# Expert rows by indirect transfers and transposes instead of one-hot products

## The chip, the core and the metric

The kernel runs on one core of one Trainium2 chip. The metric is device time in microseconds (us) of one execution; the median of three runs before is 2757.31 us (2755.22 to 2757.72). The engines are TensorE (PE; PEld is its weight load), VectorE (DVE), ScalarE (ACT), GpSimd (POOL) and SyncE (SP), which issues nearly all transfers. PSUM is the memory that PE writes to; SBUF is the on-chip memory that all engines read and write.

## What is computed

The reference runs two transformer layers (`first_block`) and then a hybrid layer. Each of the first two has a hierarchical mixture of experts (MoE) on 512 tokens of D = 1024, with 32 experts in 4 groups, hidden size 256, and two experts for each token:

```python
g_logits = (t @ w_rg) + b_rg                     # 4 groups
g_sel = argmax(g_logits); g_p = softmax(g_logits)[g_sel]
e_prob = softmax(e_logits[rows, g_sel])          # 8 experts of that group
top_p, top_i = top_k(e_prob, 2)
gates = g_p * top_p / sum(top_p)
...
hid = silu(xb @ w_gate[e]) * (xb @ w_up[e])      # xb: the rows of t sent to expert e
ys  = (hid @ w_down[e]) * slot_gate
out = segment_sum(ys, slot_tok)                  # back to the tokens
```

`t` is the RMS-normed hidden state. The rest of the model (attention, the gate behind the MoE, the last layer) is not touched by the change.

## The kernel before

Slots and groups. `moe_route` (L935) works out, for each token and each of its two experts, a slot number ("position"); blocks of 64 slots belong to one expert. The first 33 blocks are taken in 17 groups of two blocks (the last has one); two groups make a pair `u` of 256 slots. Blocks past those go through `moe_overflow` (L1349), a loop that makes no passes with these inputs; but its entry is a place where all engines meet.

Getting the rows. `router` leaves four scaled tiles `xg`, and for each a high and a low part `hs` (ACT's `copyH`, DVE's `subL`; for tiles 2 and 3 the latter at L1055, at the end of the routing). For a pair, `gather_oh` (L1133) makes a one-hot `OH` (DVE, four tiles of 128 tokens x 256 slots, two operations each, L1145 and L1146). `gather_rows(u, kk)` (L1166) multiplies `hs` by it: 16 products of 256 columns into a PSUM tile "z", copied by ACT to `X` (L1178), which has the rows turned (features on partitions, slots on columns). Four of these make a pair.

Steps. `moe` (L1059) runs a list of steps: an "up" multiplies X by the gate and up weights of a group (16 f32 products, `mm<-wu,X` in the trace), a "down" by its down weights (8 f32 products of 512 columns, `z<-wh,hid` or `z<-raw,hid`). After the first few, ups are odd steps and downs even ones. In between stand small jobs that `at(step, ...)` puts ahead of a step: the gates of a pair (`gather_gates`, PSUM tag "tp"), the transposes of its one-hots (`back`, "tp"), the transposes of the hidden state (`hidden`, "tp"), a quarter of `gather_rows`, and `combine` (L1222), which multiplies a down's outputs by turned one-hots into the PSUM tag "o", after which DVE adds it to the hidden state (L1230). "tp" and "o" have one buffer each, "z" two. Two combines stand ahead of each step from step 6 on. The order of PE, ACT, DVE and POOL in this part is the order in which the code is written; nothing reorders it:

```python
with self.tc.manual_schedule(engines={ET.PE, ET.Activation, ET.DVE, ET.Pool}):
    for s in range(N + 8):
        for f in todo.pop(s, ()):
            f = f()
            if callable(f):
                f()
        if s < N and steps[s]:
            work(s)
```

Behind each product step `rows` puts ACT's copy (L240) and DVE's subtraction (L253), which split a down's output in high and low parts. The expert weights come by SP's queue in the order of the program, into a ring of six 1 MB tiles ("wu") and the rings "wh" and "raw"; a load waits until PE has used the tile's last content. The first of them behind the loop's entry is L1114.

Of the kernel before, what the change touches and what calls it, by code (L numbers as in the profile page):

```python
# [12 lines left out]
I32 = mybir.dt.int32  # L13
AF = mybir.ActivationFunctionType
# [91 lines left out]
class Kern:  # L106
# [756 lines left out]

    def router(self, l, xs):
# [16 lines left out]
        hs = []  # L881
# [27 lines left out]
        def then(c, tt):  # L909
# [25 lines left out]
    def moe_route(self, l, xs):  # L935
# [19 lines left out]
        for tt in (2, 3):  # L955
            self.after(nc.scalar.activation(hs[tt][0], xg[tt], AF.Copy, scale=r[:, tt:tt + 1]), first)
# [68 lines left out]
        G = self.t("gates", [128, 4, 4], bufs=1)  # L1025
        v.reduce_sum(G[:, :, 2:4].rearrange("p t i -> p i t"), Ef, axis=AX.X)

# [25 lines left out]
        last = v.tensor_sub(GHL[:, :, 1], d, GHL[:, :, 0].bitcast(F32))  # L1053
        for tt in (2, 3):
            self.after(v.scalar_tensor_tensor(hs[tt][1], xg[tt], r[:, tt:tt + 1], hs[tt][0].bitcast(F32), op0=OP.mult,  # L1055
                                              op1=OP.subtract), last)
        return hs, G, GHL, oe, it

    def moe(self, l, xs):  # L1059
# [19 lines left out]
        hs, G, GHL, oe, it = self.moe_route(l, xs)  # L1079
# [49 lines left out]
        OHs, GSs, Xs, SG, Y, OHT, HID, PS = {}, {}, {}, {}, {}, {}, {}, {}  # L1129
# [4 lines left out]

        def gather_oh(u, tt):

            if tt == 0:
                pr = G[:, :, 2:4]
                if u > 0:
                    pr = self.small([128, 4, 2])  # L1140
                    nc.vector.tensor_scalar(pr, G[:, :, 2:4], -256.0 * u, None, op0=OP.add)
                OHs[u] = self.F4([128, 4, 256], F32R, "g"), pr
            OH, pr = OHs[u]
            io = self.c["iota"]
            v.tensor_scalar(OH[:, tt], io, pr[:, tt, 0:1], None, op0=OP.is_equal)  # L1145
            v.scalar_tensor_tensor(OH[:, tt], io, pr[:, tt, 1:2], OH[:, tt].bitcast(F32), op0=OP.is_equal, op1=OP.add)  # L1146

# [872 lines left out]
```

## Time and profile before

| | |
|---|---|
| median of 3 runs | 2757.31 us |
| profiled execution, device time | 2758.76 us |
| its span | 2756.7 us |
| mean granted TensorE clock | 0.975 of 2.4 GHz |
| PE / DVE / ACT / POOL busy | 2602.7 / 1338.8 / 1002.9 / 318.6 us |
| moved by transfers | 383.55 MB, mean 139 GB/s |

The MoE's expert steps take about 478 to 810 us of the span in the first layer and 1342 to 1670 in the second. The page gives busy times over the whole span; the tables of stretches and the timelines below are of single places in the expert steps, where the limits can be seen. A row of a timeline gives start, length, engine, line, operation, output<-input, count, and in brackets the idle time before it and what ended that.

### The profile page before, as it was taken

The page shows a single profiled execution, that of the slowest core. Times are in us where ns is not written, and L with a number is a line of the kernel's source. Part 1 is how long each engine was busy: PE and PEld are TensorE (multiplying, and loading weights), DVE is VectorE, ACT ScalarE, POOL GpSimd, SP SyncE. Part 2 cuts the span into 40 slices and gives each one's busy share as a digit, 9 for nine tenths or more (in the row PEclk, how much of TensorE's full clock was granted, in tenths as well). Part 3 has the DMA queues.
Part 4 walks back from the last instruction along what each step waited for, and adds up shares of the span by engine and source line. Part 5 has one row for each costly group of instructions (what it writes and reads, how often), then busy time and mean ns, then how long its engine had stood idle before and what let it go on. Part 6 is the DMA issues. An engine that isn't in the chain of part 4 may idle for free. (4 is left out here: it accounts for less than half of the span.)

```text
span 2756.7 us, 37138 instructions
## 1 busy us (share of the span) xinstructions
PE 2602.7 (94%) x14711; PEld 2000.0 (73%) x14711; DVE 1338.8 (49%) x2557; ACT 1002.9 (36%) x1840; POOL 318.6 (12%) x381
## 2 busy tenths in 40 slices
PE   7989998999999988999799999899999999999998
PEld 6777786555559777789455557777776688888898
DVE  6786535233357687644433336654356612533323
ACT  4654333211134564433111115444554522322222
POOL 0120011000000121012000001110003552011101
PEclk9999998999999999999899999999998999999999
DMA  5111336788833211223798853322121233233321
GB/s 170 54 54 62 87 126 209 291 326 314 327 114 115 77 46 47 86 93 123 268 341 314 332 210 116 119 71 60 49 73 58 89 95 119 85 99 92 96 92 66
DMA packets 224769, 383.55 MB, mean 139 GB/s; under 512 B 19658, under 2 KB 162599, under 8 KB 224592
## 3 DMA queue, kind: packets, MB, share of 16 engines
q1 hardware_dynamic: 224592, 381.13, 40.8%
q8 instruction: 118, 1.93, 0.3%
q14 instruction: 59, 0.48, 0.1%
HBM read 374.23 MB, written 6.85 MB: 138 GB/s over the span
## 5 line engine op out<-in xcount | busy, mean ns | idle before, releaser
L253 DVE TENSOR_TENSOR wh<-raw,wh 128x1024 fp32r<-128x1024 f32 (+1 forms) x251 | 304.5, 1214 | 468.7 <-ACT wh L240 464.3
L285 PE MATMUL mm<-f,wh 128*128 128x512 f32 x1296 | 525.8, 407 | 5.9 <-DVE q L251 4.7
L287 PE MATMUL mm<-f,wh 128*128 128x512 f32 x1296 | 512.5, 396 | 0.0
L286 PE MATMUL mm<-f,wh 128*128 128x512 f32 x1296 | 512.2, 395 | 0.0
L240 ACT ACTIVATE wh<-raw 128x1024 fp32r<-128x1024 f32 (+1 forms) x278 | 290.1, 1046 | 450.5 <-PE mm L286 284.6
L285 PEld LDWEIGHTS mm<-f,wh 128*128 128x128 f32 x1296 | 246.4, 190 | 72.1 <-issue 11.1
L287 PEld LDWEIGHTS mm<-f,wh 128*128 128x128 f32 x1296 | 246.0, 190 | 52.3 <-issue 0.5
L286 PEld LDWEIGHTS mm<-f,wh 128*128 128x128 f32 x1296 | 246.8, 190 | 45.9 <-issue 1.0
L1062 PE MATMUL mm<-wu,X 128*64 128x512 f32 x928 | 205.8, 596 | 0.0
L1062 PE MATMUL z<-g,o 128*128 128x256 f32 (+1 forms) x1152 | 153.9, 288 | 17.8 <-DVE g L1146 17.8
L1062 PEld LDWEIGHTS z<-g,o 128*128 128x128 f32 x1152 | 146.3, 194 | 22.1 <-DVE g L1146 18.0
L1062 PEld LDWEIGHTS mm<-wu,X 128*64 128x64 f32 x928 | 64.0, 137 | 120.4 <-issue 118.1
L1062 PE MATMUL o<-q,g 128*128 128x512 f32 x448 | 129.7, 411 | 5.7 <-DVE q L1230 5.3
L1230 DVE TENSOR_TENSOR q<-q,o 128x512 f32<-128x512 f32 x112 | 76.6, 684 | 105.5 <-PE o L1062 105.5
L1062 PEld LDWEIGHTS o<-q,g 128*128 128x128 f32 x448 | 75.7, 188 | 55.2 <-issue 34.1
L285 PE MATMUL mm<-wh,q 128*128 128x256 f32 x384 | 111.2, 290 | 3.7 <-ACT q L240 3.7
L1200 DVE SCALAR_TENSOR_TENSOR gs<-gs,mm 128x256 f32<-128x256 f32 x32 | 13.5, 422 | 205.7 <-ACT gs L444 205.7
L287 PE MATMUL mm<-wh,q 128*128 128x256 f32 x384 | 109.2, 284 | 2.7 <-POOL q L253 2.6
L286 PE MATMUL mm<-wh,q 128*128 128x256 f32 x384 | 108.5, 283 | 0.0
L253 POOL TENSOR_TENSOR wh<-raw,wh 128x1024 fp32r<-128x1024 f32 (+1 forms) x27 | 80.4, 2987 | 182.6 <-ACT wh L240 182.6
L1178 ACT COPY X<-z 128x512 f32<-128x512 f32 (+1 forms) x72 | 40.5, 563 | 156.3 <-PE z L1062 156.3
L253 DVE TENSOR_TENSOR q<-z,q 128x1024 fp32r<-128x1024 f32 x32 | 39.2, 1225 | 109.7 <-ACT q L240 109.7
(444 smaller groups left out, 4833.5 us busy)
## 6 DMA issues: line engine op xcount, KB each, us to landing
raw<-in_w_in_dram SPq DMA_DIRECT2D x142, 512.0 KB
wu<-in_w_exp_gate_dram SPq DMA_DIRECT2D x116, 512.0 KB
wu<-in_w_exp_up_dram SPq DMA_DIRECT2D x116, 512.0 KB
wh<-in_w_exp_down_dram SPq DMA_DIRECT2D x76, 512.0 KB
raw<-in_w_exp_down_dram SPq DMA_DIRECT2D x56, 512.0 KB
raw<-in_w_gu_dram SPq DMA_DIRECT2D x44, 512.0 KB
raw<-in_w_down_dram SPq DMA_DIRECT2D x20, 512.0 KB
raw<-in_w_o_dram SPq DMA_DIRECT2D x16, 512.0 KB
```

The lines of the kernel that those rows point to most:

```text
L240: nc.scalar.activation(o, i, AF.Copy, scale=scale)
L253: e.tensor_sub(o, i, h)
L285: mm(ps, aH, bH, start=first, stop=False, skip_group_check=True)
L286: mm(ps, aH, bL, start=False, stop=False, skip_group_check=True)
L287: mm(ps, aL, bH, start=False, stop=last, skip_group_check=True)
L1062: mm = lambda *a, **k: nc.tensor.matmul(*a, **k, skip_group_check=True)
L1178: return lambda: nc.scalar.copy(Xs[u][:, kk * 2:kk * 2 + 2, 0:n], pz[:, :, 0:n])
L1200: v.scalar_tensor_tensor(sg[r], sg[r], 1.0, pa[r, 0], op0=OP.add, op1=OP.mult)
L1230: return lambda: v.tensor_add(xs[tt][:, cs], xs[tt][:, cs], po)
```

## The change

`hs` is now a tile of 512 rows x 1024 in DRAM. `row_tile` scales `xg` with ACT into a tile and writes it there through POOL's queue (four times 512 KB for a layer). `row_numbers` multiplies the one-hots by the column of token numbers (8 f32 products of one column for a pair, into the tag "tp"), and DVE casts the result to integers. `row_gather` lets POOL fetch 128 rows of 4 KB by that list (an indirect transfer) into an SBUF tile, and `turned(g)` turns them with 8 transposes into a "z" tile, which ACT copies to `X` in one operation. The high and low parts and their DVE subtractions are gone. One-hots and gathers of the first pair are issued inside `moe_route`, right behind the positions, those of the second pair ahead of the overflow loop; later pairs' one-hots at steps 4u-8 and 4u-7, their row numbers and gathers at 4u-6, the turns at 4u-2 and 4u. The one-hots move from the SBUF tag "g" to "o". The overflow loop gathers in the same new way.

```diff
+    def row_tile(self, tt):
+        lt, r, rows, xg = self.routed
+        t = self.F4([128, 8, 128], tag="o")
+        i = self.nc.scalar.activation(t, xg[tt], AF.Copy, scale=r[:, tt:tt + 1])
+        self.nc.gpsimd.dma_start(rows[tt * 128:tt * 128 + 128, :], t.rearrange("p k c -> p (k c)"))
+        return i
+
+    def row_numbers(self, OH, n):
+        pi = self.pst("tp", [128, 2], 1)
+        for p in range((n + 127) // 128):
+            m = min(128, n - 128 * p)
+            for tt in range(4):
+                self.nc.tensor.matmul(pi[0:m, p:p + 1], OH[:, tt, p * 128:p * 128 + m].bitcast(F32),
+                                      self.c["slot"][:, tt:tt + 1], start=p == 0 and tt == 0, stop=tt == 3,
+                                      skip_group_check=True)
+        ix = self.small([128, 2], U32)
+        if n >= 128:
+            self.nc.vector.tensor_copy(ix[:, 0:n // 128], pi[:, 0:n // 128])
...
+    def row_gather(self, rows, ix, p, n):
+        t = self.F4([128, 1024], tag="o")
+        self.nc.gpsimd.indirect_dma_start(t[0:n], None, rows, bass.IndirectOffsetOnAxis(ap=ix[0:n, p:p + 1], axis=0))
+        return t
...
-                hs.append([self.F4([128, 8, 128], F32R, "o") for _ in range(2)])
                 if tt < 2:
-                    self.copyH(hs[tt][0], xg[tt], "act", r[:, tt:tt + 1])
-                    self.subL(hs[tt][1], xg[tt], hs[tt][0], "dve", r[:, tt:tt + 1])
+                    self.row_tile(tt)
...
         v.reduce_sum(G[:, :, 2:4].rearrange("p t i -> p i t"), Ef, axis=AX.X)
+        then()
...
-        last = v.tensor_sub(GHL[:, :, 1], d, GHL[:, :, 0].bitcast(F32))
-        for tt in (2, 3):
-            self.after(v.scalar_tensor_tensor(hs[tt][1], xg[tt], r[:, tt:tt + 1], hs[tt][0].bitcast(F32), op0=OP.mult,
-                                              op1=OP.subtract), last)
+        v.tensor_sub(GHL[:, :, 1], d, GHL[:, :, 0].bitcast(F32))
...
+        def gather_rows(u):
+            n = 64 * sum(ne(g) for g in (2 * u, 2 * u + 1) if g < NG)
+            ix = self.row_numbers(OHs[u][0], n)
+            for p in range((n + 127) // 128):
+                XR[2 * u + p] = self.row_gather(self.routed[2], ix, p, min(128, n - 128 * p))
+
+        def first_gather():
+            for tt in range(4):
+                gather_oh(0, tt)
+            gather_rows(0)
+        hs, G, GHL, oe, it = self.moe_route(l, xs, first_gather)
...
-        def gather_rows(u, kk):
-            OH = OHs[u][0]
-            if kk == 0:
+        def turned(g):
+            u, p = divmod(g, 2)
+            if p == 0:
                 Xs[u] = self.t("X", [128, 8, 256])
-            n = 128 * min(2, NG - 2 * u)
-            pz = self.pst("z", [128, 2, 256], 2)
-            for k in range(2):
-                for hl in range(2):
-                    for tt in range(4):
-                        mm(pz[:, k, 0:n], hs[tt][hl][:, kk * 2 + k], OH[:, tt, 0:n],
-                           start=k == 0 and hl == 0 and tt == 0, stop=hl == 1 and tt == 3)
-            return lambda: nc.scalar.copy(Xs[u][:, kk * 2:kk * 2 + 2, 0:n], pz[:, :, 0:n])
+            n = 64 * ne(g)
+            pz = self.pst("z", [128, 8, n], 2)
+            for k in range(8):
+                nc.tensor.transpose(pz[:, k], XR[g][0:n, k * 128:k * 128 + 128], self.ident[0:n, 0:n])
+            return lambda: nc.scalar.copy(Xs[u][:, :, p * 128:p * 128 + n], pz)
...
         for u in range(9):
-            for x in range(4):
-                if u:
-                    at(max(4 * u - 4 + x, 1), lambda u=u, x=x: gather_rows(u, x))
-                if x < 2 and 2 * u + x < NG:
+            for x in range(2):
+                if 2 * u + x < NG:
+                    if u:
+                        at(4 * u - 2 + 2 * x, lambda u=u, x=x: turned(2 * u + x))
                     at(max(4 * u - 2 + x, 1 + x), lambda u=u, x=x: back(u, x))
         back_rows(1)
-        for u in range(1, 9):
+        for u in range(2, 9):
             for tt in range(4):
-                at(4 * u - 6 + tt // 2, lambda u=u, tt=tt: gather_oh(u, tt))
+                at(4 * u - 8 + tt // 2, lambda u=u, tt=tt: gather_oh(u, tt))
+            at(4 * u - 6, lambda u=u: gather_rows(u))
+        for tt in range(4):
+            gather_oh(1, tt)
+        gather_rows(1)
         self.moe_overflow(l, xs, hs, G, it, oe)
...
-        for tt in range(4):
-            gather_oh(0, tt)
-        for kk in range(4):
-            gather_rows(0, kk)()
+        turned(0)()
         gather_gates(0)()
+        turned(1)()
```

**Place one:** PE between an up and the next down, at a step 4u-2 of the steady part of the first layer. The names are the program's tiles: `o_` is a combine's PSUM tile, `tp_` the one-buffer tag, `z_` first the block that becomes X and in the last row the down, `q_` the outputs of downs, `g_` one-hots. Before:

```order
L1062 MATMUL o_5020<-q_4839,g_4714 128x512
...
L1062 MATMUL o_5020<-q_4946,g_4714 128x512
L1188 MATMUL tp_5027<-c_all_79,g_4812 128x128 x4
L1062 MATMUL z_5033<-g_4812,o_3979 128x256
L1062 MATMUL z_5033<-g_4812,o_4027 128x256
...
L1062 MATMUL z_5033<-g_4812,o_4144 128x256
L1062 MATMUL o_5051<-q_4839,g_4714 128x512
...
L1062 MATMUL o_5051<-q_4946,g_4714 128x512
L1062 MATMUL z_5064<-wh_4691,hid_4985 64x512
```

After (here `o_4715`, a source, is an SBUF tile with gathered rows and `o_4591`, `o_4801` are one-hots; L879 is in `row_numbers`, L1215 in `turned`):

```order
L1090 MATMUL o_4884<-q_4741,g_4648 128x512
...
L1090 MATMUL o_4884<-q_4824,g_4648 128x512
L1215 MATMUL z_4891<-c_all_79,o_4715 128x128 x8
L1226 MATMUL tp_4902<-c_all_79,o_4591 128x128 x4
L1090 MATMUL o_4908<-q_4741,g_4648 128x512
...
L1090 MATMUL o_4908<-q_4824,g_4648 128x512
L879 MATMUL tp_4914<-c_all_79,o_4801 128x1 x8
L1090 MATMUL z_4929<-wh_4625,hid_4849 64x512
```

Sixteen products between the two combines have given way to eight transposes, and the row numbers of the pair after next stand between the second combine and the down.

**Place two:** PE between that down and the next up; the names as above, `mm_` the up, the second `tp_` of each the turned hidden state. Before:

```order
L1062 MATMUL z_5064<-wh_4829,hid_4985 64x512
L1062 MATMUL o_5085<-q_4839,g_4714 128x512
...
L1062 MATMUL o_5085<-q_4946,g_4714 128x512
L1188 MATMUL tp_5091<-c_all_79,g_4812 128x128 x4
L1062 MATMUL z_5097<-g_4812,o_3979 128x256
...
L1062 MATMUL z_5097<-g_4812,o_4144 128x256
L1062 MATMUL o_5115<-q_4839,g_4714 128x512
...
L1062 MATMUL o_5115<-q_4946,g_4714 128x512
L1208 MATMUL tp_5125<-c_all_79,gs_5016 128x128 x2
L1062 MATMUL mm_5130<-wu_4899,X_4909 64x512
```

After:

```order
L1090 MATMUL z_4929<-wh_4731,hid_4849 64x512
L1090 MATMUL o_4950<-q_4741,g_4648 128x512
...
L1090 MATMUL o_4950<-q_4824,g_4648 128x512
L1226 MATMUL tp_4956<-c_all_79,o_4591 128x128 x4
L1090 MATMUL o_4962<-q_4741,g_4648 128x512
...
L1090 MATMUL o_4962<-q_4824,g_4648 128x512
L1246 MATMUL tp_4968<-c_all_79,gs_4880 128x128 x2
L1090 MATMUL mm_4973<-wu_4779,X_4890 64x512
```

Between these two combines nothing is left but the four transposes of one-hots. At steps 4u the turns stand in the same way between up and down, with no row numbers; at the odd step behind it the gates' eight products stand ahead of the first combine, and the two combines follow each other directly.

**Place three:** SP at the entry of the overflow loop of the first layer, with the semaphores that each row waits for (`DMAHW` lanes are those of SP's transfers, `DMASW` lanes those of POOL's; the printed list is cut at the right). Before:

```order
L1125 DMA wh_4525<-in_w_exp_down_dram 128x1024 [waits DMAHW5_49]
L1357 TENSOR_LOAD ovt_4281 [waits DVE_49]
L1359 COMPARE_AND_BRANCH
L1359 UNCONDITIONAL_BRANCH [waits SP_sequencer_49,DMAHW0_49,DMAHW1_49,DMAHW2_49,DMAHW3_49,DMAHW6_49,DMAHW7_49]
L1359 UNCONDITIONAL_BRANCH [waits DMAHW0_49,SP_sequencer_49,DMAHW1_49,DVE_sequencer_49,DMAHW2_49,PE_sequencer_49,DMAHW3_49,Activation_sequencer_49,DMAHW4_49,Pool_sequencer_49,DMAHW5_49,DVE_49,DMAHW6_49,PE_49,DMAHW7_49,Activation_49,Pool
```

After:

```order
L1179 DMA wh_4524<-in_w_exp_down_dram 128x1024 [waits DMAHW5_49]
L1179 DMA wh_4529<-in_w_exp_down_dram 128x1024 [waits DMAHW6_49]
L1398 TENSOR_LOAD ovt_4280 [waits DVE_49]
L1400 COMPARE_AND_BRANCH
L1400 UNCONDITIONAL_BRANCH [waits SP_sequencer_49,DMAHW0_49,DMAHW1_49,DMAHW2_49,DMAHW3_49,DMAHW4_49,DMAHW7_49]
L1400 UNCONDITIONAL_BRANCH [waits DMASW4_49,DMASW3_49,DMASW5_49,DMASW2_49,DMASW6_49,DMASW1_49,DMASW7_49,DMASW0_49,DMAHW0_49,SP_sequencer_49,DMAHW1_49,DVE_sequencer_49,DMAHW2_49,PE_sequencer_49,DMAHW3_49,Activation_sequencer_49,DMAHW4_49
```

The wait of SP's last row has gained the eight lanes of POOL's transfers. On POOL itself the four writes of rows and the four gathers of the first two pairs stand ahead of this entry in the after order, where before nothing but the multiplications of the router stood.

## Rows read from the trace of the kernel before

**Rows 1.** The page, costliest groups: busy us, mean ns | idle before, releaser.

```profile
L1062 PE MATMUL z<-g,o 128*128 128x256 f32 (+1 forms) x1152 | 153.9, 288 | 17.8 <-DVE g L1146 17.8
```

**Rows 2.** Table of stretches: us, busy PE PEld DVE ACT POOL, PEclk, DMA share, GB/s.

```profile
600.00:640.00 40.00, 40.00 (x219) 22.71 (x219) 13.30 (x28) 7.72 (x13) 0.00 (x0) 1.00 0.87 323
630.00:640.00 10.00, 10.00 (x57) 5.76 (x54) 2.19 (x4) 1.94 (x3) 0.00 (x0) 1.00 1.00 364
1420.00:1430.00 10.00, 10.00 (x57) 6.09 (x58) 3.94 (x9) 1.98 (x3) 0.00 (x0) 1.00 1.03 415
```

**Rows 3.** Timeline of PE, steady part of the first layer.

```profile
572.44 1.19 PE L1062 MATMUL o<-q,g 128*128 128x512 f32 x4
573.47 0.60 PE L1188 MATMUL tp<-c_all,g 128*128 128x128 f32 x4
573.83 2.13 PE L1062 MATMUL z<-g,o 128*128 128x256 f32 x16
575.80 1.09 PE L1062 MATMUL o<-q,g 128*128 128x512 f32 x4
576.82 3.65 PE L1062 MATMUL z<-wh,hid 128*64 128x512 f32 x16
...
583.76 1.08 PE L1062 MATMUL o<-q,g 128*128 128x512 f32 x4
...
592.01 1.21 PE L1062 MATMUL o<-q,g 128*128 128x512 f32 x4
...
594.94 1.08 PE L1062 MATMUL o<-q,g 128*128 128x512 f32 x4
...
599.53 1.05 PE L1062 MATMUL tp<-ghl,g 128*128 128x6 f32 x8
600.45 1.18 PE L1062 MATMUL o<-q,g 128*128 128x512 f32 x4
```

**Rows 4.** Timeline at the same place, ACT and DVE.

```profile
580.54 1.03 ACT L240 ACTIVATE q<-z 128x1024 fp32r<-128x1024 f32 x1 [3.96 <-PE z L1062]
...
582.74 0.68 DVE L1230 TENSOR_TENSOR q<-q,o 128x512 f32<-128x512 f32 x1
...
593.42 0.68 DVE L1230 TENSOR_TENSOR q<-q,o 128x512 f32<-128x512 f32 x1
```

**Rows 5.** Timeline of PE, tail of the steps, no block between the combines.

```profile
794.76 1.19 PE L1062 MATMUL o<-q,g 128*128 128x512 f32 x4 [1.88 <-DVE q L1230]
```

**Rows 6.** Timeline of PE, early steps.

```profile
485.87 1.05 PE L1062 MATMUL tp<-ghl,g 128*128 128x6 f32 x8
...
492.11 7.09 PE L1062 MATMUL mm<-q,X 128*64 128x512 f32 x32
```

**Rows 7.** Timeline of DVE, SP and PE at the start of the steps.

```profile
461.51 0.42 DVE L1026 TENSOR_REDUCE gates<-g 128x8 f32<-128x256 f32 x1
...
462.47 2.47 DVE L1055 SCALAR_TENSOR_TENSOR o<-tmp,small,o 128x1024 fp32r<-128x1024 f32 x2
...
466.61 0.61 DVE L1145 TENSOR_SCALAR g<-c_all,gates 128x256 fp32r<-128x256 f32 x2 [1.67 <-issue]
...
468.46 0.87 DVE L1146 SCALAR_TENSOR_TENSOR g<-c_all,gates,g 128x256 fp32r<-128x256 f32 x2
...
465.29 0.35 SPq L1114 DMA_DIRECT2D wu<-in_w_exp_gate_dram  x1
...
467.67 1.41 PE L1062 MATMUL z<-g,o 128*128 128x256 f32 x4 [8.87 <-DVE g L1146]
...
478.86 3.65 PE L1062 MATMUL mm<-raw,X 128*64 128x512 f32 x16
```

**Rows 8.** Table of stretches, where the granted clock rises.

```profile
473.00:474.00 1.00, 1.00 (x9) 1.00 (x9) 0.00 (x0) 0.33 (x1) 0.00 (x0) 0.81 1.05 430
```

**Rows 9.** Timeline of SP's queue and of ACT, a load of twice 512 KB.

```profile
791.78 0.82 SPq L259 DMA_DIRECT2D raw<-in_w_ple_dram  x2
...
795.50 1.06 ACT L240 ACTIVATE wh<-raw 128x1024 fp32r<-128x1024 f32 x1 [2.65 <-DMA raw<-in_w_ple_dram]
```

More of the change, by code (lines that the diff above doesn't have):

```diff
@@ L928, in then, with moe_route @@
                 self.rstd(s, D, r[:, tt:tt + 1])
-                hs.append([self.F4([128, 8, 128], F32R, "o") for _ in range(2)])
                 if tt < 2:
-                    self.copyH(hs[tt][0], xg[tt], "act", r[:, tt:tt + 1])
-                    self.subL(hs[tt][1], xg[tt], hs[tt][0], "dve", r[:, tt:tt + 1])
+                    self.row_tile(tt)
         return then
-    def moe_route(self, l, xs):
+    def moe_route(self, l, xs, then):
         A, nc = self.A, self.nc
@@ L955, in moe_route @@
         for tt in (2, 3):
-            self.after(nc.scalar.activation(hs[tt][0], xg[tt], AF.Copy, scale=r[:, tt:tt + 1]), first)
+            self.after(self.row_tile(tt), first)
         ps = self.mmps([128, 4, 36])
@@ L1023, in moe_route @@
         v.tensor_mul(Ef, Ef, V[:, None].to_broadcast([128, 2, 4, 32]))
-        G = self.t("gates", [128, 4, 4], bufs=1)
+        G = self.positions = self.t("gates", [128, 4, 4], bufs=1)
         v.reduce_sum(G[:, :, 2:4].rearrange("p t i -> p i t"), Ef, axis=AX.X)
+        then()
         ge, gp, es = c16(), c4(), c4()
@@ L1078, in moe, with gather_oh @@
                         IN[g, i, 2 * c + k] = t[:, :, k]
-        hs, G, GHL, oe, it = self.moe_route(l, xs)
+        OHs, XR = {}, {}
+        def gather_oh(u, tt):
+            if tt == 0:
+                pr = self.positions[:, :, 2:4]
+                if u > 0:
+                    pr = self.small([128, 4, 2])
+                    nc.vector.tensor_scalar(pr, self.positions[:, :, 2:4], -256.0 * u, None, op0=OP.add)
+                OHs[u] = self.F4([128, 4, 256], F32R, "o"), pr
+            OH, pr = OHs[u]
+            io = self.c["iota"]
+            v.tensor_scalar(OH[:, tt], io, pr[:, tt, 0:1], None, op0=OP.is_equal)
+            v.scalar_tensor_tensor(OH[:, tt], io, pr[:, tt, 1:2], OH[:, tt].bitcast(F32), op0=OP.is_equal, op1=OP.add)
+        def gather_rows(u):
[8 more added lines that the diff above has]
+        hs, G, GHL, oe, it = self.moe_route(l, xs, first_gather)
         steps, up, dn = [], {}, {}
@@ L1133, in at @@
             todo.setdefault(max(s, 0), []).extend(fs)
[L1135 to L1146, printed above, removed]
         def gather_gates(u):
@@ L1370, in moe_overflow @@
                 v.scalar_tensor_tensor(OH[:, tt], io, pr[:, tt, 1:2], OH[:, tt].bitcast(F32), op0=OP.is_equal, op1=OP.add)
-            pg = self.pst("o", [64, 4], 1)
+            pg = self.pst("o", [64, 5], 1)
             for tt in range(4):
-                mm(pg, OH[:, tt].bitcast(F32), G[:, tt, 0:4], start=tt == 0, stop=tt == 3)
+                mm(pg[:, 0:4], OH[:, tt].bitcast(F32), G[:, tt], start=tt == 0, stop=tt == 3)
+                mm(pg[:, 4:5], OH[:, tt].bitcast(F32), self.c["slot"][:, tt:tt + 1], start=False, stop=tt == 3)
+            ix = self.small([128, 2], U32)
+            v.tensor_copy(ix[0:64, 0:1], pg[:, 4:5])
+            rows = self.row_gather(hs, ix, 0, 64)
             gs = self.small([64, 4])
@@ L1384, in moe_overflow @@
             for k in range(8):
-                for hl in range(2):
-                    for tt in range(4):
-                        mm(pz[:, k], hs[tt][hl][:, k], OH[:, tt], start=k + hl + tt == 0, stop=hl == 1 and tt == 3)
+                nc.tensor.transpose(pz[:, k], rows[0:64, k * 128:k * 128 + 128], self.ident[0:64, 0:64])
             nc.scalar.copy(X, pz)
```

11 lines of the change are left out of this document (8 added, 3 removed).

## The prediction

> **What bounds the kernel now.** I read the page's costliest groups first: on TensorE (PE) the products with the one-hots that the change removes take 153.9 us for 1152 instructions [rows 1]. That invites subtracting them. Next the table of stretches, for what limits the expert stage: in 600 to 640 us PE is busy in all of 40.00 us at full clock while the DMA engines work 0.87 of the time at 323 GB/s [rows 2]. So PE's order of work sets the pace, and the transfers follow not far behind. Third, the timeline of PE over two steps up and two down, which is one pair of groups: from the combine behind one up to that behind the next 19.6 us (572.44 to 592.01) [rows 3], so 39 a pair. What to see in it is where the removed block sits. It is always between two combines (o<-q,g), which share one PSUM buffer: the second must wait until VectorE (DVE) has added the first. Fourth, DVE's and ScalarE's (ACT) rows at the same place, for when that add ends [rows 4], and the tail, where the block is absent and PE is seen to wait [rows 5].
>
> **Removed and added on PE.** Per layer 9 pairs of 64 products go, 576. Sixteen take 1.97 us (573.83 to 575.80) [rows 3], 0.123 each: 70.8 us per layer. Added: 136 turns, priced by four transposes of one-hots, 0.36 us, 0.09 each [rows 3]: 12.2 us; and the row numbers, 8 small f32 products per gather of 128 rows. What f32 costs is seen on the step down: the code has 8 products, the row says x16 [rows 3], so each runs twice. The nearest row for a one-hot as weights and few columns is the gates' block, 8 in 0.92 us (599.53 to 600.45) [rows 3], 0.115 each; the transposes say 0.09 and the removed products 0.123. I take 0.115: 16 instructions, 1.84 us, for each pair of blocks, 15.6 us per layer. On paper PE sheds 43.0 us per layer, 86 us in all. The rest of this part is why I don't believe it.
>
> **Between up and down, even steps 4u.** Before: combine 592.01, block, second combine 594.94 [rows 3], 2.93 us apart. The first combine's add runs behind the step's two gate operations: 593.42, 0.68 long, ended 594.10 [rows 4]. Without the block the second combine could start at 594.16; the new turns (8 x 0.09 = 0.72) fit below that. Gain 0.78 us. Six such steps in the steady part: -4.7.
>
> **Between up and down, even steps 4u-2.** Before: 3.36 us apart (572.44 to 575.80) [rows 3]; with the add's end as floor, as above 2.15 us behind the first, the second combine is 1.2 earlier and ends at 575.6. But here the row numbers follow. They need the one-buffer PSUM tag of the turned one-hots, free when ACT has copied X (1.03 us by its copy of 128x1024 [rows 4]) and then the one-hots (half the columns, by that some 0.6): turns end 574.2, so ACT is done at 575.85. Then 1.84 us, and the step down starts at 577.74 instead of 576.82: +0.92. What was hidden is now in line.
>
> **After a step down, odd steps.** Here ACT's copy (1.03) and DVE's subtraction of the step's output stand ahead of the add on DVE, which ends at 583.42 [rows 4]; the second combine starts at 583.76 [rows 3]. So 2.0 us of products disappear and 0.26 us is gained (0.08 of the 0.34 goes for the handover): the wait was there already, covered. In the odd steps that also hold the gates, four small DVE operations more stand in that chain, and I take nothing. The tail shows the wait bare: 1.88 us of idle PE between two combines after a down, released by that add [rows 5]. Per step with row numbers +0.92-0.26 = +0.66, six times +4.0; the one even step without them (the last pair has one gather) -1.2-0.26 = -1.5. **Steady part: -4.7+4.0-1.5 = -2.2 us per layer.**
>
> **Early steps, no combines yet.** From the end of the first up (485.87 [rows 6]) to the end of the fourth. Before the second up, 32 products are gone (the 6.24 us from there to 492.11 [rows 6] become gates 0.92, a wait seen as 0.86, transposes 0.36, some 2.2): -4.0. Ahead of the first down, turns, two transposes and row numbers queue on that one PSUM tag, each behind ACT's copy: about +1.0. The next three gaps lose 16 products each but keep the same queue: -0.6, -1.2, -0.2. Together -5.0.
>
> **The start.** Before: the positions are ready at 461.93, two subtractions fill DVE to 464.94, SP's first expert load goes out at 465.29, DVE makes the one-hots until 469.33, and the first up starts at 478.86 after 64 products [rows 7]. After: subtractions off DVE's queue bring the positions 1.0 us forward (2.47 for two [rows 7]; one of the first two tiles' stood among the logits' own DVE work; bounds 0 and 1.2), 460.9. One-hots of the first pair 2.72 (466.61 to 469.33), of the second the same, each followed by what remains of its row numbers and the cast to integers, 1.6 (ten products of the sixteen stand behind the last one-hot, slower since the clock here is at the lower of its two levels, 1.2 GHz; the stretch in which it rises, 0.81 granted [rows 8], comes 5.5 us after PE began to work without a break at 467.67 [rows 7]): 460.9+2.72+1.6+0.3+2.72+1.6 = 469.8. Then GpSimd's (POOL) queue fetches. The entry of the overflow loop, with no passes, is a meeting of all engines, and SP there now waits for the eight lanes of POOL's transfers: so nothing of the expert steps, and no expert load, starts before the last gather has landed. Nothing before shows an indirect transfer. The nearest row is a load of twice 512 KB on SP's queue, 3.7 us from issue to use (791.78 to 795.50) [rows 9]; the last two gathers are twice 512 KB too, rows of 4 KB by an index list. Bounds 3.7 and, one after the other, 7.4; I take 5.0 since two of the four were issued 4.6 us earlier: 474.8. Meeting 1.7 (the idle time ahead of DVE's first operation after it [rows 7]), turns, gates and turns at half clock 3.9: first up at 480.4, 0.8 us longer for the clock, ends 488.2. Before 485.87: **+2.3 us.** SP's loads restart 11 us late, but the first 8 MB (8.4 million bytes) need 20 us at 415 GB/s [rows 2], until 497; the first down, which wants the last of them, starts after 501.
>
> The Trainium skill has a fit for such transfers (DMA: Bandwidth & Descriptors, section Anatomy of one DMA — SWDGE (gpsimd) path): 2.0 us and the bytes at 436 GB/s, which would be 3.2 us for 512 KB, and the start would come out 1.8 us sooner than with my 5.0; no run here shows it for an index list.
>
> **What is free.** Writing the rows (four transfers of 512 KB per layer by POOL) lies behind the routing that ends with the positions; in the steady part a gather is issued four steps, some 39 us, ahead of its turn, ten times the 3.7 us row. Each pair asks for 1.05 MB more beside 12.6: 13.6 MB in 39 us is 350 GB/s, below the 364 at which the engines are full in the first layer [rows 2]. If that cover went and the rate stayed at today's 323, a pair would take 42 us, 3 more than now.
>
> **Sum.** 2.3-5.0-2.2 = -4.9 us per layer, -9.8 in two. The profiled run took 2758.76 us (span 2756.7): 2749.0. The median of the runs shown is 2757.31, 1.45 less: **2747.5 us.** Bounds: gathers -1.3/+2.4, positions -0.2/+1.0, row numbers -3.0/+1.0 per layer: 2738 to 2756.
>
> **Rivals.**
> *The row numbers run once* (D): 0.92 us for 1.84 in seven places and 0.7 twice at the start, -7.8 per layer: 2732. Against: every f32 product in the timeline is doubled; for: transposes, also f32, are not.
> *The waits don't take the place of the products* (C): the add ends sooner, say because ACT is less loaded, and PE sheds its 43 us. A pair would fall to 34.3 us and need 397 GB/s; the second layer reached 415, the first 364 [rows 2], which holds that layer at 37.4 us per pair. Gain 43+16: 2698. Against: 1.88 us of bare waiting [rows 5]. The Trainium skill (DMA: Bandwidth & Descriptors, section Where 436 GB/s comes from) puts the binding limit from HBM at about 358 GB/s; then both layers would stop near 38.1 us and C would end at 2736. The row of 415 GB/s disagrees.
> *The gathers are served one at a time ahead of the loop* (B, slower): POOL makes a list of 128 transfers for each, and if each takes s us to land before the next moves, the entry is at 465.2+4s instead of 474.8. From s = 3.6 the change gains nothing, from 4.3 it is slower by 0.2%; at s = 6 it is +14.4 per layer: 2776. For it: no transfer before goes by an index list or by POOL's queue, so no row excludes it; against: two plain loads together took 3.7 [rows 9].
> *It does not do what it says*: the order shows all 576 products gone, so this has no chance worth a number.
>
> **How the numbers follow.** Forecast 0.57, D 0.12, C 0.06, B 0.13, and 0.12 for mixtures. About 0.2% (5.5 us) is what a measurement here tells from no change, so faster means below 2751.8: 0.40 of the forecast's 0.57 lies there, 0.17 within; with D, C and 0.03 of the mixtures faster is 0.61, same 0.22, slower 0.17. The range 2732 to 2766 takes in the forecast's bounds and D, a part of B, and leaves out C and B's upper part.
>
> **What would show it.** In the profile after: PE idle between two combines released by the DVE add (steady part right); row numbers as x16 at about 0.1 us (x8: D); distance up to up some 39.0 us (34 to 37: C); the first up at 480 (later than 485: B), and SP's first expert load near 475. Wrong would be a PE that is full in the steady part with the pair unchanged, or DMA share at 1.00 throughout.

## The result and the profile after

The changed kernel takes 2793.22 us (median of 4 runs, 2789.19 to 2795.65) against 2756.79 us for the kernel before (4 runs): ratio 1.0131, 95% interval 1.0114 to 1.0149. It is 36 us slower where 10 us faster was forecast, and lies far outside the range of 2732 to 2766 us. The page of its profile (busy us, mean ns | idle before, releaser; then issues with KB and median us to landing):

```profile
span 2791.7 us, 36037 instructions
PE 2572.6 (92%) x14103; PEld 1933.5 (69%) x14103; DVE 1332.1 (48%) x2567; ACT 994.5 (36%) x1802; POOL 350.2 (13%) x423
L1090 PE MATMUL o<-q,g 128*128 128x512 f32 x448 | 140.2, 437 | 49.1 <-DVE q L1268 48.2
L893 POOL DMA_INDIRECT o<-rows,small x34 | 32.0, 941 | 571.7 <-DVE small L884 394.2
...
o<-rows,small POOLq DMA_INDIRECT x34, 7.2
```

PE is busy 2572.6 us, 30 less than before, in a span 35 us longer, and the mean granted clock is 0.958 where it was 0.975. The combines now have 49.1 us of idle PE ahead of them, 48.2 of it released by DVE's add; before it was 5.7:

```profile
L1062 PE MATMUL o<-q,g 128*128 128x512 f32 x448 | 129.7, 411 | 5.7 <-DVE q L1230 5.3
```

A gather occupies POOL 0.94 us and lands 7.2 us after its issue (median, beside the weight stream). The products of [rows 1] are gone.

One pair of groups in the steady part, PE's timeline (start, length, operation, count, idle before and its releaser), to be laid beside [rows 3] and the row that ends the same pair before, which comes first:

```profile
611.82 1.21 PE L1062 MATMUL o<-q,g 128*128 128x512 f32 x4
```

```profile
578.97 1.20 PE L1090 MATMUL o<-q,g 128*128 128x512 f32 x4
...
581.23 1.17 PE L1090 MATMUL o<-q,g 128*128 128x512 f32 x4
582.63 1.95 PE L879 MATMUL tp<-c_all,o 128*128 128x1 f32 x16 [0.22 <-ACT g L1227]
584.51 3.65 PE L1090 MATMUL z<-wh,hid 128*64 128x512 f32 x16
588.09 1.21 PE L1090 MATMUL o<-q,g 128*128 128x512 f32 x4
...
591.16 1.22 PE L1090 MATMUL o<-q,g 128*128 128x512 f32 x4 [1.43 <-DVE q L1268]
592.53 7.09 PE L1090 MATMUL mm<-wu,X 128*64 128x512 f32 x32
599.55 1.20 PE L1090 MATMUL o<-q,g 128*128 128x512 f32 x4
...
601.70 1.19 PE L1090 MATMUL o<-q,g 128*128 128x512 f32 x4
...
607.32 1.18 PE L1090 MATMUL o<-q,g 128*128 128x512 f32 x4
610.33 2.06 PE L1090 MATMUL o<-q,g 128*128 128x512 f32 x4 [1.83 <-DVE q L1268]
612.19 0.63 PE L1246 MATMUL tp<-c_all,gs 128*128 128x128 f32 x2
612.75 7.58 PE L1090 MATMUL mm<-wu,X 128*64 128x512 f32 x32
620.26 1.21 PE L1090 MATMUL o<-q,g 128*128 128x512 f32 x4
```

From the end of one up to the end of the next but one, which is one pair, it now takes 41.3 us (578.97 to 620.26) for 39.4 (572.44 in [rows 3] to 611.82). All the waits that the prediction named are there: 2.15 us between the combines of a step 4u, behind an up (599.55, 601.70; forecast 2.15), 3.07 and 3.01 behind a down, with 1.43 and 1.83 us of bare idle. What was not forecast stands at the end: the second combine at 610.33 takes 2.06 us, where combines took 1.1 to 1.2 [rows 3], the two transposes 0.63, and the up 7.58 as against 7.09. The table of stretches at that place (us, busy PE PEld DVE ACT POOL, granted clock, DMA share, GB/s):

```profile
610.00:610.50 0.50, 0.17 (x1) 0.17 (x2) 0.27 (x1) 0.00 (x0) 0.00 (x0) 0.87 1.05 418
610.50:611.00 0.50, 0.50 (x2) 0.40 (x3) 0.00 (x0) 0.00 (x0) 0.00 (x0) 0.50 1.03 410
...
614.00:614.50 0.50, 0.50 (x4) 0.14 (x2) 0.46 (x2) 0.00 (x0) 0.00 (x0) 1.00 0.57 205
```

PE stands idle from 608.5 to 610.33. In the stretch from 610.0 the granted clock falls; from 610.5 it is 0.50, the lower level of 1.2 GHz, and it is back at 1.00 only at 614. The time that the clock stays below 1.00 is called a spell in what follows. Before, no half microsecond of the expert steps, from 480 to 830 us and from 1340 to 1690, was below 1.00. In the changed kernel a spell of 3 to 7 us follows the step with the gates in five of the six pairs of each layer.

The start of the first layer, to be laid beside [rows 7] (DVE, PE, POOL, SP, PE):

```profile
457.99 0.42 DVE L1056 TENSOR_REDUCE gates<-g 128x8 f32<-128x256 f32 x1
...
466.38 2.72 PE L879 MATMUL tp<-c_all,o 128*128 128x1 f32 x12 [0.25 <-DVE o L1120]
...
470.81 0.94 POOL L893 DMA_INDIRECT o<-rows,small  x1 [0.30 <-DMA rows<-o]
...
476.57 0.33 SPq L1168 DMA_DIRECT2D wu<-in_w_exp_gate_dram  x1
...
482.33 4.50 PE L1090 MATMUL mm<-raw,X 128*64 128x512 f32 x16
...
490.20 1.05 PE L1090 MATMUL tp<-ghl,o 128*128 128x6 f32 x8
```

SP's first expert load goes out at 476.57, 5.8 us after the last gather's issue at 470.81, and the first up ends at 490.20, 4.3 us later than before although the positions (458.41) were 3.5 us earlier. By stages of the first layer: first up's end +4.3; from there to the end of the fourth up 47.45 (490.20 to 537.65) as against 47.2, +0.25; from there to the last up +9.2 (that starts 13.8 us later in all); the tail +3.0, where the last up takes 5.08 us instead of 3.65 and the last down 3.48 instead of 1.94, both with the clock at 0.50 in part. Together 16.8. The second layer is like it: +8.1 from the positions to the first up's end (first layer 7.9), +1.7, and +10.9 to the last up.

### The profile page after: what moved, and what is told of

It reads as the page before. It is cut to its first block, busy times and chain, and to the rows that moved or that the text cites. A ratio compares the mean times of both kernels' runs of the same rounds, so it can differ in the third digit from the quotient of the medians.

```text
span 2791.7 us, 36037 instructions
## 1 busy us (share of the span) xinstructions
PE 2572.6 (92%) x14103; PEld 1933.5 (69%) x14103; DVE 1332.1 (48%) x2567; ACT 994.5 (36%) x1802; POOL 350.2 (13%) x423
## 4 chain that ended last, share of the span: by engine, by line
PE 40%; DVE 6%; ACT 3%; issue 1%; POOL 1%; DMA 0%; POOLq 0%; ACTq 0%; DVEq 0%
PE mm L286 8%; PE mm L288 7%; PE mm L287 7%; PE mm L1090 5%; PE z L1090 3%; PE o L1090 1%; PE z L287 1%; PE z L286 1%; PE z L288 1%; PE o L629 1%; DVE q L254 1%; ACT q L241 1%; PE o L1645 1%; DVE tmp L359 1%; DVE wh L254 0%
## 5 line engine op out<-in xcount | busy, mean ns | idle before, releaser
L286 PEld LDWEIGHTS mm<-f,wh 128*128 128x128 f32 x1296 | 245.4, 189 | 73.9 <-issue 10.6
L287 PEld LDWEIGHTS mm<-f,wh 128*128 128x128 f32 x1296 | 245.9, 190 | 45.6 <-issue 0.7
L1090 PE MATMUL mm<-wu,X 128*64 128x512 f32 x928 | 222.5, 635 | 0.0
L1090 PE MATMUL o<-q,g 128*128 128x512 f32 x448 | 140.2, 437 | 49.1 <-DVE q L1268 48.2
L893 POOL DMA_INDIRECT o<-rows,small x34 | 32.0, 941 | 571.7 <-DVE small L884 394.2
L254 DVE TENSOR_TENSOR q<-z,q 128x1024 fp32r<-128x1024 f32 x32 | 39.2, 1224 | 119.6 <-ACT q L241 119.6
L445 ACT ACTIVATE gs<-mm 128x256 f32<-128x256 f32 x32 | 12.3, 384 | 226.0 <-PE mm L1090 226.0
L629 PE MATMUL o<-tmp,q 128*128 128x256 f32 x576 | 81.2, 285 | 2.9 <-DVE tmp L254 2.6
```

Of the source, the lines that this page charges most:

```text
L254: e.tensor_sub(o, i, h)
L286: mm(ps, aH, bH, start=first, stop=False, skip_group_check=True)
L287: mm(ps, aH, bL, start=False, stop=False, skip_group_check=True)
L629: self.nc.tensor.matmul(po, v[kt // 2][:, x, kt % 2, vc], w[y][:, kt, :], start=x + y + kt == 0, stop=y == 1 and kt == nk - 1, skip_group_ ...
L893: self.nc.gpsimd.indirect_dma_start(t[0:n], None, rows, bass.IndirectOffsetOnAxis(ap=ix[0:n, p:p + 1], axis=0))
L1090: mm = lambda *a, **k: nc.tensor.matmul(*a, **k, skip_group_check=True)
```

## The experiments

Theory 1: between two combines PE waits for DVE's add whether or not there is work; the removed products covered that wait, and without them the clock falls behind it. The row numbers, in line, and the start add their own. Theory 2: the gathers and row writes disturb the weight stream. Theory 3: the row numbers are the whole loss. Ratios below are to the kernel before, with 95% intervals; differences to the changed kernel are to its median of 2793.22. The kernel before came out at 2755.0 to 2756.8 us beside the groups of experiments, so a difference of under 2 us says nothing. The traces of three runs show executions 6 to 8 us below their medians (row numbers moved, 2748.76 us; row numbers and turns moved, 2734.49; add first, 2741.24), so other executions of these kernels may hold more spells than are counted here.

**Filling the bare waits of the changed kernel.**

```diff
...
+        for u in range(2, 9):
+            for s in (4 * u - 3, 4 * u - 1):
+                if s > 6:
+                    at(s, lambda u=u: filler(u, 12))
```

`filler(u, m)`, left out here, issues m products of one-hots by one-hots into a "z" tile that nothing reads.

> The changed kernel, with 12 products of one-hots by one-hots (their result is not used) put between the two combines of each odd step from step 7 on, where PE now stands idle 1.43 or 1.83 us. Theory 1 (the idle wait itself costs little, but after it the granted clock falls to its lower level for 3 to 7 us once per pair, which makes the second combine 0.9, the transposes 0.25 and the up 0.45 us longer): more work, less time; the spells of 0.50 in the steady part vanish, the pair goes from 41.3 to about 39.7 us, the kernel from 2793 to about 2771. Theory 2 (PE is delayed by the gathers' and writes' transfers): no change, 2790 to 2796, or a little slower. Theory 3 (the loss is the row numbers standing in line): no change either.

Measured: 2782.59 us (1.0103, 1.0076 to 1.0130), 10.6 less for more work. PE's timeline:

```profile
582.38 1.95 PE L879 MATMUL tp<-c_all,o 128*128 128x1 f32 x16 [0.22 <-ACT g L1235]
584.25 5.35 PE L1090 MATMUL z<-wh,hid 128*64 128x512 f32 x16
...
609.76 1.59 PE L1090 MATMUL z<-o 128*128 128x256 f32 x12
611.76 1.19 PE L1090 MATMUL o<-q,g 128*128 128x512 f32 x4 [0.41 <-DVE q L1276]
...
613.10 7.09 PE L1090 MATMUL mm<-wu,X 128*64 128x512 f32 x32
```

Behind the gates' step the up is back at 7.09, as theory 1 says. But in six of the ten pairs with sixteen row numbers the spell has moved: it now follows these, and the down takes 5.35 us for 3.65 (such a pair 41.4 us, one without a spell 39.7). So only half of the expected gain came. Filling the waits alone is no cure while the row numbers stand in line.

**Gathers of the second pair behind the loop's entry.** `gather_rows` now makes the row numbers and returns the call that issues the gathers.

```diff
...
-        gather_rows(1)
+        fetch = gather_rows(1)
         self.moe_overflow(l, xs, hs, G, it, oe)
+        fetch()
```

> The changed kernel, with the two gathers of the second pair issued behind the entry of the overflow loop (their row numbers stay ahead of it). If the meeting of the engines waits for the last gather (its issue 470.8, the meeting's end 476.6 in the first layer): the first expert load goes out near 471.5 and the first up starts near 477, 4 to 5 us earlier per layer, the kernel near 2784. If something else ends last there (the row numbers of the second pair, 469.1, or the loads of the first groups), 0 to 2 us per layer, 2789 to 2793.

Measured: 2781.20 us (1.0096, 1.0069 to 1.0124), 12.0 less.

```profile
471.04 0.33 SPq L1171 DMA_DIRECT2D wu<-in_w_exp_gate_dram  x1
...
476.90 5.56 PE L1090 MATMUL mm<-raw,X 128*64 128x512 f32 x16
```

SP starts at 471.04, 13.2 us behind the positions (457.84 in this run) as against 18.2 in the changed kernel. The meeting at the loop did wait for the last gather.

**Row numbers moved into the odd steps**, between the two combines, and from the PSUM tag "tp" to "z".

```diff
...
+            if u > 1:
+                at(4 * u - 5, lambda u=u: gather_rows(u))
...
-            at(4 * u - 6, lambda u=u: gather_rows(u))
```

> The changed kernel, with the row numbers of a pair and its gathers moved from between the second combine and the down of step 4u-6 to between the two combines of step 4u-5, into the other PSUM tag. Theory 3 (row numbers in line: the down starts 5.54 us behind the up instead of 4.38): that distance falls to about 3.2, the step after the down grows by 0.3, the pair falls by 2.1 to 39.2 and the kernel to about 2766, with the clock's falls behind the gates' steps as before. Theory 1 alone (only the clock): the pair 41.3 to 40.7, 2785. Theory 2 (transfers): no change.

Measured: 2756.29 us (1.0001, 0.9989 to 1.0014): 36.9 less, all of the loss and more than any of the three theories had said.

```profile
602.44 1.19 PE L1090 MATMUL o<-q,g 128*128 128x512 f32 x4 [1.83 <-DVE q L1268]
...
603.78 8.78 PE L1090 MATMUL mm<-wu,X 128*64 128x512 f32 x32
```

The wait behind the gates' step is still 1.83 us. Here the combine behind it stays at 1.19 and the clock falls a little later, in the up. Pairs with a spell take 39.0 to 39.3 us, those without 37.5 to 37.6, and half of the twelve are now without. The gain is larger than the row numbers' own 2.1 us per pair: spells went too. Taken alone, this run would fit theory 3 as well; the run with DVE's add ahead, below, decides it, since it gains more with the row numbers still in line.

**The kernel before, with most products left out.** Seven of eight products of each output are left out; no gather, no row numbers, no writes.

```diff
-                for hl in range(2):
-                    for tt in range(4):
-                        mm(pz[:, k, 0:n], hs[tt][hl][:, kk * 2 + k], OH[:, tt, 0:n],
-                           start=k == 0 and hl == 0 and tt == 0, stop=hl == 1 and tt == 3)
+                mm(pz[:, k, 0:n], hs[0][0][:, kk * 2 + k], OH[:, 0, 0:n], start=k == 0, stop=True)
```

> The kernel before, with one of the eight products of each output of a gather left out of none and seven left out of eight (the experts get wrong rows): 504 of 576 products less per layer, no indirect transfer, no row numbers, no row writes. By the products' pace alone 62 us per layer go: 2633. Theory 1 (the combines wait for DVE's adds and the clock falls behind the bare waits): the pair goes from 39.4 to 37 to 39 us and shows spells of 0.50; 7 us per layer less at the start, 4 in the early steps; the kernel near 2726. Theory 2 (the changed kernel's loss is that of its transfers): no spells of 0.50, pair 35 to 37, 2660 to 2700.

Measured: 2714.39 us (0.9841, 0.9814 to 0.9868). Of some 124 us of PE work (504 products of 0.123 us in each layer) 41 came off the time; theory 1 had said 30, the products' pace alone all of it.

**The same, but with the odd steps' products left in.**

```diff
...
+                if u > 1 and kk % 2:
+                    for hl in range(2):
+                        for tt in range(4):
+                            mm(pz[:, k, 0:n], hs[tt][hl][:, kk * 2 + k], OH[:, tt, 0:n],
+                               start=k == 0 and hl == 0 and tt == 0, stop=hl == 1 and tt == 3)
+                else:
+                    mm(pz[:, k, 0:n], hs[0][0][:, kk * 2 + k], OH[:, 0, 0:n], start=k == 0, stop=True)
```

> The kernel before with seven of eight products left out as in the run of that kind, except that the blocks in the odd steps (between a down and the next up, from the second pair on) keep all their 16 products; the experts get wrong rows. It does 196 products more per layer than that run, 24 us of PE by the pace. Theory 1 (there the products stood in a wait that is there anyway, and keep the clock up): no spell of 0.50 in the steady part, pair near 37.4, the kernel 2700 to 2712, not above the 2714 of the run with less work. If PE's work counts: 2714 + 2 x 24 = 2762, or 2740 if half is hidden.

Measured: 2708.55 us (0.9837, 0.9820 to 0.9853). PE's timeline of the run with less work, then of this one:

```profile
592.03 2.08 PE L1062 MATMUL o<-q,g 128*128 128x512 f32 x4 [1.60 <-DVE q L1227]
...
594.46 7.53 PE L1062 MATMUL mm<-wu,X 128*64 128x512 f32 x32
```

```profile
584.86 1.98 PE L1062 MATMUL z<-g,o 128*128 128x256 f32 x16
586.85 1.21 PE L1062 MATMUL o<-q,g 128*128 128x512 f32 x4
...
588.21 7.09 PE L1062 MATMUL mm<-wu,X 128*64 128x512 f32 x32
```

With 48 us more of PE work it is not slower (the medians differ by 5.8 us in its favour, the intervals overlap). The thin one has the bare wait and the spell here (2.08 and 7.53 us), with no transfer added anywhere; this one has neither. So theory 2 isn't needed for the spells. But the thin one's spells are few: its bare wait is some 1.6 us in every pair, and behind it the clock falls in two of six pairs of the first layer and in one of six of the second. Here it does not fall:

```profile
630.99 1.19 PE L1062 MATMUL o<-q,g 128*128 128x512 f32 x4 [1.60 <-DVE q L1227]
```

Its pairs without a spell take 37.4 us, and all pairs of the run with more work 37.6. So 28 products more, 3.4 us of PE by their pace, cost 0.2 us where they stood; the spells that they kept away make up for that.

**Row numbers moved, and the gates' steps filled.**

```diff
+        for u in range(3, 9):
+            at(4 * u - 3, lambda u=u: filler(u, 12))
```

> The kernel of the run with the row numbers moved, with 12 products of one-hots by one-hots (not used) between the two combines of each step with the gates (4u-3, from u = 3 on), the only place where its PE still stands idle for 1.8 us. Clock theory: the spells of 0.50 in the steady part go, all pairs take the 37.5 us that this kernel already shows where no spell falls (those with a spell 39.2), 6 to 7 us per layer, the kernel near 2743. Transfers theory (a pair at 37.5 needs 363 GB/s): pairs stay at 38 to 39 with PE waiting for wu or wh, 2750 to 2756.

Measured: 2742.49 us (0.9956, 0.9939 to 0.9973), as theory 1 said to a microsecond. No spell is left between 560 and 700 us, and the pairs take 37.5 to 37.7 us in both layers.

**Row numbers and turns moved**, useful work in place of the filling; then with the late gathers as well.

```diff
-                        at(4 * u - 2 + 2 * x, lambda u=u, x=x: turned(2 * u + x))
+                        at(4 * u - 3 if u > 1 and x == 0 else 4 * u - 2 + 2 * x, lambda u=u, x=x: turned(2 * u + x))
```

> The kernel with the row numbers moved, and in addition the eight transposes of a pair's first gather moved from between the combines of step 4u-2 to those of step 4u-3 (the one with the gates), where PE idles. If any work in the idle stretch keeps the clock up: as the run with products for filling, near 2743. If transposes of 0.9 us with 0.9 us of idle left do not hold it: spells as before, 2754 to 2758.

> The kernel with row numbers and turns moved, and the gathers of the second pair issued behind the loop's entry. The late gathers gave 12 us alone, at another place of the program: 10 to 12 us below the run without them, that is 2732 if the turns hold the clock, 2744 if not. If the early steps then wait for the second pair's rows (the gather lands before its turn by some 10 us only), 2740 to 2750.

Measured: 2740.20 us (0.9952, 0.9937 to 0.9968) and 2736.90 us (0.9927, 0.9911 to 0.9944).

```profile
597.01 1.20 PE L1090 MATMUL o<-q,g 128*128 128x512 f32 x4 [0.94 <-DVE q L1268]
```

In the first of the two, 0.94 us of idle are left ahead of the second combine of the gates' step, and the up behind it is at full clock; pairs without a spell take 37.5 us. The late gathers add 3.3 us here where they gave 12 alone; the two intervals overlap, and from the positions to SP's first load the second run is again 5 us shorter (13.0 and 18.4). Part of the rest shows in the two traces: the last pair of each layer takes 40.3 and 40.4 us in the second run, with spells of 7 us, and 39.0 and 37.5 us in the first. The remainder stays open.

**Row numbers in one pass**: as f32r products, with the token numbers rounded into a tile of two equal columns (`self.slots`).

```diff
...
-                self.nc.tensor.matmul(pi[0:m, p:p + 1], OH[:, tt, p * 128:p * 128 + m].bitcast(F32),
-                                      self.c["slot"][:, tt:tt + 1], start=p == 0 and tt == 0, stop=tt == 3,
+                self.nc.tensor.matmul(pi[0:m, p], OH[:, tt, p * 128:p * 128 + m], self.slots[:, tt], start=p == 0 and tt == 0, stop=tt == 3,
...
```

> The changed kernel with the row numbers as f32r products (8 instructions for 16, two equal columns of token numbers in a rounded copy). Theory: 0.9 us less in line ahead of the down in seven places per layer, and 2 to 3 us less at the start of each layer, where 32 of them run at the lower clock: 2793 to 2775 or so, the spells of 0.50 behind the gates' steps stay. If the row numbers cost nothing in line: 2790 to 2794.

Measured: 2781.92 us (1.0097, 1.0080 to 1.0114), 11.3 less, somewhat under the 18 expected.

```profile
617.28 1.05 PE L879 MATMUL tp<-slots,o 128*128 128x2 f32 x8 [0.23 <-ACT g L1228]
```

x8 in 0.98 us (the down starts at 618.26) for x16 in 1.88 (582.63 to 584.51 in the changed kernel). The spells remain, as said.

**DVE's add ahead of its subtraction**, in the changed kernel and in the kernel before.

```diff
...
                     rows(g, 0)
-                    rows(g, 1)
+                    if 6 <= s + 1 <= 33:
+                        late.append(lambda: rows(g, 1))
+                    else:
+                        rows(g, 1)
...
-            return lambda: v.tensor_add(xs[tt][:, cs], xs[tt][:, cs], po)
+            def add():
+                v.tensor_add(xs[tt][:, cs], xs[tt][:, cs], po)
+                while late:
+                    late.pop(0)()
+            return add
```

> The changed kernel with DVE's subtraction of a down's output put behind the add of the first combine of the step after it, where it stood ahead. If the second combine's wait is for DVE's order of work: the idle stretches of 1.43 and 1.83 us shrink to 0.2 to 0.7, the odd steps become 1.2 us shorter each, the spells behind the gates' steps go (they may come back behind the row numbers, as in the run with filling): pair 41.3 to 38.5 or 40, the kernel 2755 to 2778. If the wait is for the products' end or ACT's copy: no change, 2790 to 2796.

> The kernel before with the same exchange on DVE (add first, then the subtraction). Theory: the products between the combines cover that wait entirely, so PE stays full and nothing moves: 2753 to 2757, pair 39.4 to 39.1. If DVE's order costs time there too: 1.2 us per odd step, 2730.

Measured: 2747.64 us (0.9974, 0.9964 to 0.9985) for the changed kernel, 45.6 less than it; 2755.74 us (1.0000, 0.9991 to 1.0010) for the kernel before. The changed kernel, then the kernel before:

```profile
586.64 1.19 PE L1090 MATMUL o<-q,g 128*128 128x512 f32 x4 [0.34 <-DVE q L1270]
...
604.73 1.20 PE L1090 MATMUL o<-q,g 128*128 128x512 f32 x4 [0.78 <-DVE q L1270]
...
606.07 7.09 PE L1090 MATMUL mm<-wu,X 128*64 128x512 f32 x32
```

```profile
581.55 2.13 PE L1062 MATMUL z<-g,o 128*128 128x256 f32 x16
583.51 1.08 PE L1062 MATMUL o<-q,g 128*128 128x512 f32 x4
```

The same exchange of two DVE operations is worth 46 us in one kernel and nothing in the other. In the changed kernel the waits shrink from 1.43 and 1.83 to 0.34 and 0.78, the up behind them is 7.09, and no spell is left between 560 and 660 us; a pair takes 37.6 us for 41.3. Of these 3.7 us, 2.1 are the two waits themselves and 1.6 the spell. In the kernel before the products fill the time whichever comes first (a pair 39.2 us for 39.4). This shows theory 1's wait directly, and it answers theory 3, since the row numbers still stand in line. The gain was larger than expected since no spell came back behind them.

**All together** (row numbers and turns moved, one pass, late gathers, add first):

> Row numbers and turns moved into the odd steps, gathers of the second pair behind the loop's entry, row numbers in one pass, and DVE's add ahead of its subtraction. By PE's floors a pair falls from 37.5 to 35.5, which needs 384 GB/s. If the transfers hold that rate: 2 us per pair below the 2737 of the run without the last two edits, and 2 us per start: near 2707. If they are full at the 364 seen in the first layer before: that layer stays at 37.4 per pair, the second goes to 35.5, near 2720, and PE waits for wu or wh.

Measured: 2714.20 us (0.9853, 0.9836 to 0.9869), 41 us below the kernel before and 79 below the changed one. It beats both. The table of stretches:

```profile
560.00:600.00 40.00, 39.40 (x194) 18.66 (x191) 13.47 (x29) 7.10 (x11) 1.87 (x2) 1.00 1.00 388
...
1400.00:1440.00 40.00, 38.88 (x192) 19.43 (x192) 15.66 (x33) 7.75 (x12) 1.87 (x2) 1.00 1.00 389
```

Here PE is busy 39 of 40 us at full clock and the DMA engines are full, at 388 GB/s; a pair takes 35.6 us. All gathers and row writes are still there, so at 41.3 us a pair they were no limit: that speaks against theory 2. The 35.6 us are what the expectation gave by PE's own work (35.5), so the 364 GB/s at which [rows 2] shows a DMA share of 1.00 were no limit.

## Why the prediction was wrong

**The wait between the combines: right.** The prediction said that the products cover a wait for DVE's add, with floors of 2.15 and some 3.1 us. Measured 2.15, 3.07 and 3.01; the exchange on DVE confirms the cause. Steps 4u gained 0.67 for the forecast 0.78, the odd steps 0.29 and 0 for 0.26 and 0.

**The row numbers: right in kind, a little short.** They run as x16, 0.117 us each for 0.115, and stand in line as said. The down of step 4u-2 starts 1.16 us later than before (5.54 behind the up, 4.38 in [rows 3]) for +0.92, because the products wait for ACT another 0.2 us. Rival D, row numbers that run once, did not happen.

**The steady sum: the step that failed.** The prediction priced idle PE at its length and left the clock at 1.00. The row that it read for a bare wait, 1.88 us in the tail [rows 5], has no fall behind it, and nothing looked for one: the granted clock belonged in the sum of any edit that thins PE's work. Per pair: 0.88 us on the second combine, 0.25 on the transposes, 0.49 on the up, together 1.6; with +1.16-0.67-0.29+0.14 for the rest (0.14 is the second combine behind the down, 1.22 us for 1.08) that makes the measured +1.9 us, where the forecast had -0.1. Five such pairs take 1.8 to 3.4 us more each, 11.0 together; the sixth, which has no spell and half the row numbers, takes 1.0 less and the way from there to the last up 0.8 less. That is the +9.2 us of this stretch, for which the forecast said -2.2.

**The early steps: wrong by the same term.** -5.0 forecast, +0.25 measured. The chain on the one PSUM tag was foreseen; that the clock falls in it was not. PE's timeline at the first down:

```profile
502.81 2.00 PE L879 MATMUL tp<-c_all,o 128*128 128x1 f32 x16 [1.13 <-ACT g L1227]
...
506.22 3.68 PE L1090 MATMUL z<-wh,hid 128*64 128x512 f32 x8 [0.46 <-ACT hid L1248]
509.68 2.74 PE L1090 MATMUL z<-raw,hid 128*64 128x512 f32 x8
...
529.47 8.26 PE L1090 MATMUL mm<-wu,X 128*64 128x512 f32 x32
```

The down takes 6.1 us (its successor starts at 512.35) instead of 3.6, and the fourth up 8.26 instead of 7.09.

**The start: right in mechanism, wrong in three terms, of which one made good for the others.** Forecast +2.3 us, measured +4.3. From the positions to the first up's end the forecast had 27.3 us, measured are 31.8. Row numbers at the lower clock take 0.23 us each (12 in 2.72), not 0.14, which is 1.0 us more per pair and twice in line; and from the issue of the second pair's first gather to the meeting's end it is 7.0 us (469.57 to 476.57) for 5.0, inside the bounds of 3.7 and 7.4. The two terms together are 4.0 of the 4.5 us. Against them stands the third: the positions came 3.5 us earlier for a forecast of 1.0 and bounds of 0 and 1.2. That is in part chance, for in the ten traces with the new routing they come anywhere from 455.4 to 461.8 us, in the four with the old one from 461.7 to 462.2. Rival B did not happen: a gather holds POOL for 0.94 us, the next is issued 1.24 us behind it (469.57, 470.81), and the four of the start land 4.8 us (median) behind their issue, so they overlap. The experiment with late gathers took 5 us of this away per layer.

**The tail: not in the sum.** Forecast nothing, measured +3.0 us, for two spells that fall in it (794.5 to 798.5 and 811.5 to 815.5).

**The sum.** In the first layer +4.3+0.25+9.2+3.0 = +16.8 for the forecast -4.9, a miss of 21.7 us. Adding up one minus the granted clock over half microseconds gives what the spells took: 5.1 us in the early steps, 10.2 in the steady part, 3.4 in the tail, 18.7 together. So the clock is most of the miss, and the gathers and row numbers at the start are most of the remainder. No rival held this case: each took the clock as given.

**The transfers: right.** They were free at this pace. Only the reading that the engines are full at 364 GB/s [rows 2] was wrong: a DMA share of 1.00 went with 388 GB/s in the same layer in the last experiment. The Trainium skill's fit (DMA: Bandwidth & Descriptors, section Anatomy of one DMA — SWDGE (gpsimd) path) gives an estimate of 3.2 us for 512 KB; this trace has a median of 7.2 us for gathers beside the weight stream, and 5.8 from the last one's issue to the meeting's end at the start. Its limit of about 358 GB/s (section Where 436 GB/s comes from) does not bind this core here: it moved those 388 GB/s over 40 us.

## What to carry to other kernels

Before you take work off a busy engine, ask what the next instruction behind it waits for: if that comes no sooner, the work was a free cover, and a PE that then stands idle can lose its clock as well. Here the uncovered wait alone cost nothing, since it was there before; the spell behind it cost 1.6 us a pair. Shorten the wait first (here: two DVE operations exchanged), then remove the work, and put what the new way adds into the gaps that are left. An experiment that puts useless work back is a cheap test for this.

## What the hardware showed

The granted clock fell behind 1.83 us of idle PE in most of the changed kernel's gates' steps and stayed at 0.50 for 3 to 7 us. It did not fall behind 1.43 us in the neighbouring steps, nor behind the same 1.83 us in the last pair of each layer, where the up runs at full clock (here the first layer):

```profile
775.39 1.19 PE L1090 MATMUL o<-q,g 128*128 128x512 f32 x4 [1.83 <-DVE q L1268]
...
776.73 7.09 PE L1090 MATMUL mm<-wu,X 128*64 128x512 f32 x32
```

Nor did it fall behind 1.88 us in the tail of the kernel before [rows 5], where it is 1.00 from 780 to 800 us, while behind 1.88 us in the tail of the changed kernel it did (811.5). And it fell in a down that followed 1.95 us of one-column products with hardly any idle time (5.35 us for 3.65). Idle length alone does not decide it. What does was not tried. One-column products of f32 took 0.117 us each at the full clock and 0.23 at the lower one.
